# A decoder layer on one core: one store moved to another DMA queue, one gate product moved into an earlier head, two output products cut in half

## The chip, the cores and the metric

The kernel runs on one core of a Trainium2 chip. The metric is device time in microseconds (us) for one execution of the whole layer, median of three runs. A separate execution was profiled; its trace gives the start and the length of every instruction, what each one waited for, and when DMAs were issued. In what follows PE is the matrix engine, ACT the activation engine, DVE the vector engine, POOL the general-purpose engine, and SP the engine that does nothing here but issue DMAs. POOL issues DMAs too, from a queue of its own.

## The reference, cut to what matters

One layer over 1024 tokens of width 1024, in float32: a normed input `h` is projected, three branches are computed and merged by sigmoid gates, and a channel mixer follows. What the change touches is the merge and what feeds it:

```python
proj = h @ w_in
q_d, k_d, v_d, u_p, q_m, gate_logits = split(proj)
a = diff_attention(q_d, k_d, v_d, lam)          # 8 heads, two softmax maps per head
a = rms_norm(a, subln_g) * (1.0 - lam_init)     # per head
y_attn = a @ w_attn_branch
y_pool = multiscale_pool(u_p, ...) @ w_pool_branch
y_mem  = memory_cross_attention(q_m, ...) @ w_mem_branch
gates = sigmoid(gate_logits)                    # three gates of 1024 columns
mix = gates[0] * y_attn + gates[1] * y_pool + gates[2] * y_mem
x = x + rms_norm(mix @ w_out, norm_mix_post)    # then the channel mixer
```

## The kernel before, in words

Every float32 product is made of three matmuls of "high" and "low" parts (`mm3`, L94). A weight that comes from memory as `raw` is split into such parts by one ACT copy and one DVE subtraction (`split`, L83; `wsplit`, L330, loads and splits). The tags `raw`, `wh` and `wl` have two buffers each, and the pages of `product` (L181) take turns in the last two.

The order of work: norms, memory attention, pooling; then the stretch that the code calls `gp` (L609 on), the attention heads (L1009 on), the merge (L1080 on), the output projection, and the channel mixer.

**The merged pool and memory gates, L609 to L629.** For each pair of 128 output columns (`dt` = 0, 2, 4, 6) and each of two branches, `seven` (L204) computes gate logits for both column tiles with seven half-size products instead of eight. It needs two raw weight tiles: `rawg` of the first kind has two buffers and is loaded one `seven` ahead, that of the second has one buffer and can be loaded only when the last page of the `seven` before has been split from it. The gated branch is summed into `mix`, 128x2x1024, and stored to `mixp_d` in DRAM, 1 MB each, four times in all, at L629 from POOL's queue. All loads of this stretch come from SP's queue. Right behind the last of them come the value projections (L634 to L738): `vtmp` (L639) takes a buffer of the same tag `g` as `mix`, so its first writer, the ACT copy at L703, waits until the last store of `mix` has read its source.

**The attention branch's gates.** The eight column tiles of the first gate are made in three places. Tiles 0 and 1 come from a `seven` just before attention (L766 to L768) into `g01`, which is stored at L1021 to L1023. Tile 2 has its weights split there as well (`gate2`, L770); its 48 matmuls of 128x512 are traced by the generator `gate` (L855), which pauses half way through each of two 512-token halves, evicts each half with an ACT copy (L867) and stores it from POOL (L868). One piece of 12 is taken before the first head (L1015), the other three pieces in head 0. Tile 3 is in head 7, tiles 4 to 7 behind the last head (L1089).

**Heads.** A head has four blocks of two rows of 128 queries. For each row `scores` (L877) makes two maps: matmuls into `pss` (two buffers of two banks), a DVE pass that adds the bias and finds the extreme (L901), an ACT exponential (L906). `combine` (L912) joins the maps on DVE, `turn_weights` (L925) transposes on PE and splits, `weigh_values` (L941) multiplies by the values. Heads 1 to 6 also compute the next head's keys (`head_keys`, L829, 48 matmuls of 128x512). `weave` (L259) spreads such fillers evenly over a head's stages. Head 0 has no `head_keys`; its fillers are loads and the rest of gate tile 2.

**What sets the order on an engine.** When the program is built, a planner lays out one fixed instruction order for each engine: it runs through a cost model of its own, takes what is ready in that model, and of several ready instructions the one that was traced first. So a matmul that was traced late can stand early in PE's order, in the place of a wait that the model foresaw, and a load can stand ahead of one traced before it. On the chip each engine, SP's and POOL's queues among them, keeps that order and waits at the head of it. `tc.issue_after(i)` forbids the planner to place the instructions of a block ahead of `i` on `i`'s engine; it adds no wait.

**The merge.** Behind the heads, for each head: `a` (the head's output) and `rb` (its norms, which went through DRAM as `ss_d`, `sum_d` and `r_d`) are loaded, multiplied on DVE and split into `ath` and `atl` (L1092 to L1101); the norms of heads 4 to 7 are computed at L1095, when those of heads 0 to 3 have long been known. Then for each of eight column tiles (L1119) the weights are split, 48 matmuls over all eight heads go into `pya`, and the result is gated, added to `mixp_d` and split into `mixh` and `mixl`.

Of the kernel before, what the change touches and what calls it, by code (L numbers as in the profile page):

```python
# [1 line left out]

# [36 lines left out]
def kernel(  # L39
# [298 lines left out]
    def chunk(w, c0, n=P):  # L338
        return w[:, c0:c0 + n].rearrange("(k p) c -> p k c", p=P)
# [269 lines left out]
    with tc.tile_pool(name="gp", reuse_waits="tile", bufs=2, side="right") as gp_:  # L609
        for dt in range(0, KT, 2):  # L610
            mix = None
            for b in (1, 0):
                raws = []
                for e in range(2):
                    w = (grp if e else wst).tile([P, KT, P], F32, tag="raw", name="rawg", bufs=2 - e)
                    nc.sync.dma_start(out=w, in_=chunk(w_in, C_G + (2 - b) * D + (dt + e) * P))
                    raws.append(w)
                y = gp_.tile([P, 2, S], F32, tag="y", name="y")
                nc.sync.dma_start(out=y, in_=branch_d[b][dt:dt + 2].rearrange("e p s -> p e s"))
                g = gp_.tile([P, 2, S], F32, tag="g", name="g", bufs=3)  # L620
                s12, s43 = [gq.tile([P, 2, H4, P], F32, tag="t", name="s") for _ in range(2)]
                seven(raws, (s12[:, 0], s12[:, 1], s43[:, 0], s43[:, 1]), hop, g)
                sigmoid = nc.scalar.activation(out=g, in_=g, func=AF.Sigmoid)
                nc.vector.tensor_tensor(out=g, in0=g, in1=y, op=ALU.mult)
                if b == 1:
                    mix = g
                else:
                    nc.vector.tensor_tensor(out=mix, in0=mix, in1=g, op=ALU.add)
            nc.gpsimd.dma_start(out=mixp_d[dt:dt + 2].rearrange("e p s -> p e s"), in_=mix)  # L629

# [134 lines left out]
        late = []  # L767
        channels(C_G, ss=[ss[:, j] for j in range(4)], g=g01, late=late)  # L768

        gate2 = wsplit(chunk(w_in, C_G + 2 * P), [P, KT, P])  # L770
        with tc.issue_after(gate2[2].ins):
            late[0]()
    rstack.close()
    tstack.close()
# [79 lines left out]

    def gate(dt):  # L855

        with tc.issue_after(last["load"].ins):
            wh, wl, _ = gate2 if dt == 2 else wsplit(chunk(w_in, C_G + dt * P), [P, KT, P])
        for i in range(2):
            pg = pbank(name="pg0")  # L860
            for k in range(KT):
                if k == H4:
                    yield
                last["gate"] = mm3(pg, wh[:, k, :], wl[:, k, :], hTh[i][:, k, :], hTl[i][:, k, :],
                                   k == 0, k == KT - 1)
            g = gq.tile([P, H], F32, tag="t", name="g0")
            nc.scalar.activation(out=g, in_=pg, func=AF.Copy)  # L867
            nc.gpsimd.dma_start(out=gate_d[dt][:, i * H:(i + 1) * H], in_=g)  # L868
            yield
# [7 lines left out]
    def scores(h, b, u):  # L877

        ks = kts[h]
        t = 2 * b + u  # L880
        n = (t + 1) * P
        parts = 1 if n <= H else 2
        m = n // parts
        q = qts[h, t // 4]
        ts = slice((t % 4) * P, (t % 4 + 1) * P)
        mx = small.tile([P, 2], F32, tag="mx", name="mx")
        sm = small.tile([P, 1], F32, tag="sm", name="sm")
        z2 = []

        def halves(a):  # L890
            return a.rearrange("p (a m) -> p a m", a=parts)

        for c in range(2):
            pss = bank2(name="pss2")
            for i in range(parts):
                keys = ks[c][:, i * m:(i + 1) * m]
                for j in range(2):
                    nc.tensor.matmul(pss[:, i * H:i * H + m], q[:, j, c, ts], keys, start=(j == 0), stop=(j == 1))  # L898
            z = ap_.tile([P, S], F32, tag="z%d" % c, name="z", bufs=3 - c)
            o = 896 - t * P  # L900
            nc.vector.tensor_tensor_reduce(  # L901
                out=halves(z[:, 0:n]), in0=pss.rearrange("p (a m) -> p a m", a=2)[:, 0:parts, 0:m],
                in1=halves(biases[h][:, o:o + n]), scale=1.0, scalar=3.0e38,
                op0=ALU.add, op1=ALU.min, accum_out=mx[:, c:c + 1])
            z2.append(z)
            nc.scalar.activation(out=z[:, 0:n], in_=z[:, 0:n], func=AF.Exp, scale=-1.0,  # L906
                                 bias=mx[:, c:c + 1], accum_out=sm if c else sums[:, h, t:t + 1])
        exps[h, b, u] = z2, mx, sm
        if b == 3 and u == 1:
            kts.pop(h)  # L910
# [95 lines left out]
    def steps(gen, n):  # L1006
        return [lambda: next(gen, None)] * n
# [4 lines left out]
    load_keys(0)  # L1012
    first = gate(2)
    head_bias(0)
    next(first)  # L1015
    for _ in values(0):
        pass
    queries(0, 1)
    load_keys(1)
    last["keys"] = last["load"]  # L1020
    with tc.issue_after(last["load"].ins):  # L1021
        for dt in range(2):
            nc.sync.dma_start(out=gate_d[dt], in_=g01[dt])  # L1023
    GATES = ((2,), (), (), (), (), (), (), (3,))
    blocks = [(h, b) for h in range(NH) for b in range(4)]
    for h in range(NH):
        stages = []
        for b in range(4):
            n = 4 * h + b
            if n == 0:  # L1030
                def first_scores():
                    with tc.issue_after(last["gate"].ins):
                        scores(0, 0, 0)
                stages.append(first_scores)
            else:
                stages.append(lambda h=h, b=b: scores(h, b, 0))
            if b == 1 and h + 1 < NH:
                stages.append(lambda h=h: head_bias(h + 1))
            if n >= 1:
                def weights(n=n):  # L1040
                    combine(*blocks[n - 1], 1)
                    turn_weights(*blocks[n - 1])
                stages.append(weights)
            stages.append(lambda h=h, b=b: scores(h, b, 1))
            stages.append(lambda h=h, b=b: combine(h, b, 0))
            if n >= 2:
                stages.append(lambda n=n: head_norm(*blocks[n - 2]))
            if n >= 1:
                stages.append(lambda n=n: weigh_values(*blocks[n - 1]))
            if h == HG and b == 0:  # L1050
                stages.append(lambda: turn_sums(0))
            if h == HG and b == 1:
                stages.append(lambda: load_norms(0))
            if h == HG and b == 3:
                def norms():
                    with tc.issue_after(last["combine"].ins):
                        head_norms(0)
                stages.append(norms)
            if b in (1, 3) and h + 1 < NH:
                stages.append(lambda h=h, b=b: queries(h + 1, b // 2))  # L1060
        fillers = []
        if h + 1 < NH:
            if h:
                fillers += steps(head_keys(h + 1), 4)
            for n, step in enumerate(steps(values(h + 1), 2)):
                fillers.insert(2 * n + 1, step)
        for dt in GATES[h]:
            fillers += steps(first if dt == 2 else gate(dt), 3 if dt == 2 else 4)
        weave(stages, fillers)
    combine(*blocks[-1], 1)  # L1070
    turn_weights(*blocks[-1])
# [10 lines left out]
    ath = [atp.tile([P, S], F32R, name="ath%d" % h) for h in range(NH)]  # L1082
    atl = [atp.tile([P, S], F32R, name="atl%d" % h) for h in range(NH)]

    with tc.tile_pool(name="sub", reuse_waits="tile", bufs=4, side="right") as sub:
        gs = sub.tile([P, 1], F32, name="gs", bufs=1)
        nc.vector.tensor_scalar(out=gs, in0=cols[:, 1, 44:45], scalar1=1.0 - LAM_INIT, scalar2=None,
                                op0=ALU.mult)
        for dt in range(4, KT):  # L1089
            for step in steps(gate(dt), 4):  # L1090
                step()
        for h in range(NH):  # L1092
            if h == HG:
                with tc.issue_after(ends["square"].ins):
                    head_norms(1)  # L1095
            a = sub.tile([P, S], F32, tag="a", name="a")
            nc.sync.dma_start(out=a, in_=ao_d[h])
            rb = sub.tile([P, S], F32, tag="rb", name="rb")
# [17 lines left out]
        wol.append(pool.tile([P, D], F32R, name="wol%d" % k))  # L1116
        split(woh[k], wol[k], raw)

    for dt in range(KT):  # L1119
        wh, wl, _ = wsplit(chunk(w_attn_branch, dt * P), [P, KT, P])  # L1120
        for i in range(2):
            hs = slice(i * H, (i + 1) * H)
            gm2 = gq.tile([P, 2, H], F32, tag="t", name="gm2")
            g, mp = gm2[:, 0, :], gm2[:, 1, :]
            nc.sync.dma_start(out=g, in_=gate_d[dt][:, hs])
            nc.sync.dma_start(out=mp, in_=mixp_d[dt][:, hs])
            nc.scalar.activation(out=g, in_=g, func=AF.Sigmoid)
            py = (pbank if i else bank)(name="pya")
            for k in range(KT):
                mm3(py, wh[:, k, :], wl[:, k, :], ath[k][:, hs], atl[k][:, hs], k == 0, k == KT - 1)  # L1130
            nc.vector.tensor_tensor(out=g, in0=py, in1=g, op=ALU.mult)
            nc.vector.tensor_tensor(out=g, in0=g, in1=mp, op=ALU.add)
            split(mixh[i][:, dt, :], mixl[i][:, dt, :], g)
    for k in range(4):
        load_wo(woa, k)
    dstack.close()
# [363 lines left out]
```

## Time and profile before

| what | value |
|---|---|
| median of 3 runs | 1768.14 us (1767.33 to 1770.3) |
| profiled execution, its own time | 1771.58 us |
| its span, first to last instruction | 1769.8 us |
| ACT busy | 884.6 us (50%) |
| DVE busy | 1274.3 us (72%) |
| POOL busy | 48.6 us (3%) |
| granted TensorE clock, mean over the span | 0.995 |
| DMA packets | 294.95 MB, mean 167 GB/s |

How to read what is quoted below. A line of the timeline has the start in us, the length in us, the engine, the line of the code, the operation, `out<-in` by the program's names, shape, how many were merged into it, and in brackets how long the engine had been idle and what ended that. A line of the waits has engine and line, what it waited for, then us in total, times, the longest in us. A line of the windows has a stretch, its length, the busy time (and number of instructions) of PE, PE's weight loads, DVE, ACT and POOL, the granted PE clock, the busy share of the 16 DMA engines and GB/s; where a window is restricted to one tile, only the engines that touch it are listed. Matmuls overlap, so a matmul's listed length is more than its share of PE's time; the distance between two starts is that share. A line of the DMA issues has `out<-in`, the queue, how many, KB each, and the median us from issue to landing.

### The profile page before, as it was taken

What the parts mean: (1) busy time and instruction counts of PE and PEld (TensorE: products, weight loads), DVE (VectorE), ACT (ScalarE), POOL (GpSimd) and SP (SyncE); (2) the same over time, 40 slices, a digit from 0 to 9 for tenths busy, and PEclk for the clock granted to TensorE, in tenths of its full rate; (3) what the DMA queues carried; (4) which work ended last, traced back from release to release, by engine and by line L of the source; (5) the groups of instructions that cost most, each with busy time, mean ns of one, the idle gap of its engine ahead of it and who ended that gap; (6) DMA issues with size and microseconds to landing.
All of it is one profiled execution on the core that took longest, in us unless ns stands there. A gap on an engine that the chain in (4) does not pass through costs nothing.

```text
span 1769.8 us, 22658 instructions
## 1 busy us (share of the span) xinstructions
PE 1722.2 (97%) x8138; PEld 1426.2 (81%) x8138; DVE 1274.3 (72%) x2227; ACT 884.6 (50%) x1551; POOL 48.6 (3%) x107
## 2 busy tenths in 40 slices
PE   6999999999899999999999999999999999999997
PEld 5788888777778878888888878888888888788886
DVE  7775875655566567888865557858888888878476
ACT  5434454333444467777753333545555555543452
POOL 0000000000000011111110000000000000000000
PEclk9999999999999999999999999999999999999999
DMA  7783543434784595765556481374334323583343
GB/s 243 249 315 132 180 153 131 126 129 143 228 254 144 188 250 166 192 163 157 157 177 227 157 241 72 111 234 137 108 107 125 115 76 107 185 294 105 112 143 131
DMA packets 232933, 294.95 MB, mean 167 GB/s; under 512 B 15873, under 2 KB 161526, under 8 KB 230134
## 3 DMA queue, kind: packets, MB, share of 16 engines
q1 hardware_dynamic: 228214, 281.94, 50.4%
q0 software_dynamic: 4608, 11.57, 1.8%
q8 instruction: 64, 1.05, 0.3%
q14 instruction: 47, 0.39, 0.1%
HBM read 201.62 MB, written 85.56 MB: 162 GB/s over the span
## 4 chain that ended last, share of the span: by engine, by line
PE 80%; DVE 9%; DMA 5%; ACT 3%; issue 2%; SPq 0%; DVEq 0%; ACTq 0%; POOLq 0%
PE pa L95 7%; PE pa L97 7%; PE pa L96 7%; PE pb L95 5%; PE pb L97 5%; PE pb L96 5%; PE pss L898 2%; PE poa L953 2%; PE pe L96 2%; PE pe L95 2%; PE pe L97 2%; PE pya L95 2%; PE pya L97 2%; PE pya L96 2%; PE pd L95 2%
## 5 line engine op out<-in xcount | busy, mean ns | idle before, releaser
L86 ACT ACTIVATE wpage<-s 128x512 fp32r<-128x512 f32 x136 | 85.2, 626 | 113.1 <-DVE s L194 44.6
L87 DVE TENSOR_TENSOR wpage<-s,wpage 128x512 fp32r<-128x512 f32 x136 | 92.8, 689 | 45.3 <-ACT wpage L86 45.2
L1278 DVE SCALAR_TENSOR_TENSOR cvt<-gv,cols,cvt 128x1023 f32<-128x1023 f32 x88 | 112.5, 1278 | 15.6 <-ACT cvt L1274 15.6
L901 DVE CUSTOM_DVE_ANT_0 z<-pss,hbias 128x256 f32<-128x256 f32 (+7 forms) x128 | 94.9, 753 | 27.4 <-PE pss L898 25.8
L906 ACT ACTIVATE z<-z,mx 128x256 f32<-128x256 f32 (+7 forms) x128 | 99.0, 774 | 19.8 <-DVE mx L901 19.4
L95 PE MATMUL pa<-T,wpage 128*128 128x512 f32 x264 | 102.9, 390 | 1.6 <-DVE gv L252 1.6
L96 PE MATMUL pa<-T,wpage 128*128 128x512 f32 x264 | 102.7, 389 | 0.0
L97 PE MATMUL pa<-T,wpage 128*128 128x512 f32 x264 | 102.7, 389 | 0.0
L898 PE MATMUL pss<-ks,q 128*128 128x512 f32 (+5 forms) x384 | 89.4, 352 | 1.3 <-DVE mx L901 1.1
L86 ACT ACTIVATE page<-blk 128x1024 fp32r<-128x1024 f32 (+1 forms) x42 | 41.4, 988 | 86.2 <-PE pe L96 50.6
L87 DVE TENSOR_TENSOR page<-blk,page 128x1024 fp32r<-128x1024 f32 (+1 forms) x42 | 47.6, 1133 | 38.9 <-ACT page L86 38.8
L86 ACT ACTIVATE wh<-raw 128x1024 fp32r<-128x1024 f32 (+1 forms) x46 | 41.9, 910 | 67.3 <-issue 16.5
L898 PEld LDWEIGHTS pss<-ks,q 128*128 128x128 f32 x384 | 63.3, 190 | 12.4 <-DVE mx L901 7.7
L95 PE MATMUL pa<-hT,wpage 128*128 128x512 f32 x168 | 66.3, 394 | 7.3 <-ACT wpage L86 7.3
L95 PE MATMUL pd<-page 128*128 128x512 f32 x176 | 68.6, 390 | 1.7 <-ACT row L1388 1.7
L96 PE MATMUL pd<-page 128*128 128x512 f32 x176 | 68.5, 389 | 0.0
L97 PE MATMUL pd<-page 128*128 128x512 f32 x176 | 68.5, 389 | 0.0
L97 PE MATMUL pa<-hT,wpage 128*128 128x512 f32 x168 | 66.0, 393 | 0.0
L96 PE MATMUL pa<-hT,wpage 128*128 128x512 f32 x168 | 65.9, 392 | 0.0
L953 PEld LDWEIGHTS poa<-aT,v 128*128 128x128 f32 x480 | 61.3, 192 | 3.9 <-ACT srow L973 1.6
L953 PE MATMUL poa<-aT,v 128*128 128x256 f32 (+1 forms) x480 | 64.0, 283 | 0.0
L87 DVE TENSOR_TENSOR wl<-raw,wh 128x1024 fp32r<-128x1024 f32 (+1 forms) x46 | 47.6, 1035 | 18.3 <-ACT wh L86 18.0
(416 smaller groups left out, 5056.7 us busy)
## 6 DMA issues: line engine op xcount, KB each, us to landing
q<-q_d SPq DMA_DIRECT2D x64, 256.0 KB, 5.5
wd<-in_w_down_dram SPq DMA_DIRECT2D x22, 512.0 KB, 5.2
tw_d<-wd SPq DMA_DIRECT2D x11, 1024.0 KB, 4.6
rawv<-in_w_up_dram SPq DMA_DIRECT2D x22, 512.0 KB, 5.8
rawu<-in_w_up_dram SPq DMA_DIRECT2D x22, 512.0 KB, 4.0
ff_d<-cvt SPq DMA_DIRECT2D x22, 512.0 KB, 4.4
blk<-ff_d SPq DMA_DIRECT2D x20, 512.0 KB, 7.5
br<-tw_d SPq DMA_DIRECT2D x20, 512.0 KB, 3.7
```

The lines of the kernel that those rows point to most:

```text
L86: copy = nc.scalar.activation(out=hi, in_=src, func=AF.Copy)
L87: nc.vector.tensor_tensor(out=lo, in0=src, in1=hi.bitcast(F32), op=ALU.subtract)
L95: nc.tensor.matmul(o, ah, bh, start=first, stop=False, skip_group_check=onto)
L96: nc.tensor.matmul(o, ah, bl, start=False, stop=False, skip_group_check=onto)
L97: return nc.tensor.matmul(o, al, bh, start=False, stop=last, skip_group_check=onto)
L898: nc.tensor.matmul(pss[:, i * H:i * H + m], q[:, j, c, ts], keys, start=(j == 0), stop=(j == 1))
L901: nc.vector.tensor_tensor_reduce(out=halves(z[:, 0:n]), in0=pss.rearrange("p (a m) -> p a m", a=2)[:, 0:parts, 0:m], in1=halves(biases[h][ ...
L906: nc.scalar.activation(out=z[:, 0:n], in_=z[:, 0:n], func=AF.Exp, scale=-1.0, bias=mx[:, c:c + 1], accum_out=sm if c else sums[:, h, t:t + 1])
L953: nc.tensor.matmul(po[:, qs], (vh, vl)[i][:, k, :], w[j][:, ws], start=(n == 0), stop=(n == len(terms) - 1))
L1278: nc.vector.scalar_tensor_tensor(out=cv[:, sh:], in0=u[:, 0:S - sh], scalar=w, in1=cv[:, sh:], op0=ALU.mult, op1=ALU.add)
```

## The change

Four edits.

- The store of `mix` (L629) is issued by SP instead of POOL.
- Gate tile 3 moves from head 7 to head 0, tile 4 from behind the heads to head 7, so that tiles 5 to 7 remain behind them. Tile 3's weights are loaded and split before head 0, ahead of the stores of `g01`. `gate` now pauses after every two of its eight `k`, 6 matmuls at a time; two such pieces (12 matmuls, as before) are taken before head 0.
- Each gate matmul is put behind the last matmul of the newest `scores` (`issue_after`), and the pieces are inserted among a head's fillers from the front, at every second place, instead of being appended.
- Column tiles 0 and 1 of the merge are begun over heads 0 to 3 (`merge_heads(dt, 0)`, 48 matmuls for the two) before the loop comes to head 4; the other half of each follows when all heads are there. Their four banks and two weight buffers are held in between. Tiles 2 to 7 are computed in two halves in a row.

```diff
-            nc.gpsimd.dma_start(out=mixp_d[dt:dt + 2].rearrange("e p s -> p e s"), in_=mix)
+            nc.sync.dma_start(out=mixp_d[dt:dt + 2].rearrange("e p s -> p e s"), in_=mix)
...
-        gate2 = wsplit(chunk(w_in, C_G + 2 * P), [P, KT, P])
-        with tc.issue_after(gate2[2].ins):
+        ready = {2: wsplit(chunk(w_in, C_G + 2 * P), [P, KT, P])}
+        with tc.issue_after(ready[2][2].ins):
             late[0]()
...
         with tc.issue_after(last["load"].ins):
-            wh, wl, _ = gate2 if dt == 2 else wsplit(chunk(w_in, C_G + dt * P), [P, KT, P])
+            wh, wl, _ = ready.pop(dt) if dt in ready else wsplit(chunk(w_in, C_G + dt * P), [P, KT, P])
         for i in range(2):
             pg = pbank(name="pg0")
             for k in range(KT):
-                if k == H4:
+                if k in (2, 4, 6):
                     yield
-                last["gate"] = mm3(pg, wh[:, k, :], wl[:, k, :], hTh[i][:, k, :], hTl[i][:, k, :],
-                                   k == 0, k == KT - 1)
+                with tc.issue_after(last["scores"].ins) if "scores" in last else nullcontext():
+                    last["gate"] = mm3(pg, wh[:, k, :], wl[:, k, :], hTh[i][:, k, :], hTl[i][:, k, :],
+                                       k == 0, k == KT - 1)
...
-                    nc.tensor.matmul(pss[:, i * H:i * H + m], q[:, j, c, ts], keys, start=(j == 0), stop=(j == 1))
+                    last["scores"] = nc.tensor.matmul(pss[:, i * H:i * H + m], q[:, j, c, ts], keys,
+                                                      start=(j == 0), stop=(j == 1))
...
-    next(first)
+    for _ in range(2):
+        next(first)
...
     with tc.issue_after(last["load"].ins):
+        ready[3] = wsplit(chunk(w_in, C_G + 3 * P), [P, KT, P])
         for dt in range(2):
             nc.sync.dma_start(out=gate_d[dt], in_=g01[dt])
-    GATES = ((2,), (), (), (), (), (), (), (3,))
+    GATES = ((2, 3), (), (), (), (), (), (), (4,))
...
+        n = 0
         for dt in GATES[h]:
-            fillers += steps(first if dt == 2 else gate(dt), 3 if dt == 2 else 4)
+            for step in steps(first if dt == 2 else gate(dt), 6 if dt == 2 else 8):
+                fillers.insert(min(n, len(fillers)), step)
+                n += 2
         weave(stages, fillers)
...
+    pys = {}
+
+    def merge_heads(dt, g):
+
+        if g == 0:
+            pys[dt] = wsplit(chunk(w_attn_branch, dt * P), [P, KT, P])[:2] + (bank(name="pya"), pbank(name="pya"))
+        wh, wl, *py = pys[dt]
+        for i in range(2):
+            hs = slice(i * H, (i + 1) * H)
+            for k in range(g * HG, (g + 1) * HG):
+                mm3(py[i], wh[:, k, :], wl[:, k, :], ath[k][:, hs], atl[k][:, hs], k == 0, k == KT - 1)
...
-        for dt in range(4, KT):
-            for step in steps(gate(dt), 4):
+        for dt in range(5, KT):
+            for step in steps(gate(dt), 8):
                 step()
         for h in range(NH):
             if h == HG:
                 with tc.issue_after(ends["square"].ins):
                     head_norms(1)
+
+                for dt in range(2):
+                    merge_heads(dt, 0)
...
-    for dt in range(KT):
-        wh, wl, _ = wsplit(chunk(w_attn_branch, dt * P), [P, KT, P])
-        for i in range(2):
+    def merge(dt):
+
+        for i, py in enumerate(pys.pop(dt)[2:]):
             hs = slice(i * H, (i + 1) * H)
...
-            py = (pbank if i else bank)(name="pya")
-            for k in range(KT):
-                mm3(py, wh[:, k, :], wl[:, k, :], ath[k][:, hs], atl[k][:, hs], k == 0, k == KT - 1)
             nc.vector.tensor_tensor(out=g, in0=py, in1=g, op=ALU.mult)
             nc.vector.tensor_tensor(out=g, in0=g, in1=mp, op=ALU.add)
             split(mixh[i][:, dt, :], mixl[i][:, dt, :], g)
+
+    for dt in range(KT):
+        if dt >= 2:
+            merge_heads(dt, 0)
+        merge_heads(dt, 1)
+        merge(dt)
```

More of the change, by code (lines that the diff above doesn't have):

```diff
@@ L1 @@
-from contextlib import ExitStack
+from contextlib import ExitStack, nullcontext
 import concourse.bass as bass
```

## The prediction

> **What bounds the kernel now.** I read the page's head first, then the windows of 25 us, then who PE waited for, then the timeline around each place where PE stood.
>
> ```profile
> span 1769.8 us, 22658 instructions
> PE 1722.2 (97%) x8138; PEld 1426.2 (81%) x8138; DVE 1274.3 (72%) x2227; ACT 884.6 (50%) x1551; POOL 48.6 (3%) x107
> ...
> PE pa L95 <- ACT wpage L86: 7.3, 4, 3.3
> PE ve L95 <- ACT vpage L86: 3.9, 1, 3.9
> PE pta L936 <- DVE aT L87: 1.8, 3, 0.9
> PE pn L971 <- DVE aT L87: 1.4, 1, 1.4
> ```
>
> PE is the bound. The change takes no matmul away and adds none, so it can only fill or shorten stretches in which PE waits or runs slowly. Those it touches are the first two rows of waits (around the mix stores) and the last two (head 0).
>
> ```profile
> 366.00:371.00 5.00, 5.00 (x16) 3.93 (x16) 3.21 (x6) 1.49 (x3) 0.00 (x0) 0.66 0.00 0
> 448.00:456.00 8.00, 6.59 (x15) 4.90 (x16) 4.86 (x6) 3.55 (x7) 0.00 (x0) 0.57 0.43 135
> ...
> 633.00:656.00 23.00, 22.86 (x124) 18.60 (x122) 18.27 (x53) 16.44 (x41) 2.22 (x4) 1.00 0.85 228
> 656.00:673.00 17.00, 13.57 (x84) 11.57 (x85) 13.57 (x39) 13.06 (x34) 2.68 (x5) 0.90 0.50 166
> ...
> 862.00:906.00 44.00, 43.32 (x262) 36.79 (x263) 34.07 (x81) 30.74 (x73) 6.45 (x12) 1.00 0.32 90
> 906.00:944.00 38.00, 38.00 (x170) 31.39 (x170) 24.95 (x36) 15.33 (x19) 4.32 (x8) 1.00 0.86 302
> ```
>
> Behind waits PE's granted clock drops: 5 x 0.34 = 1.7 us lost at 366, 8 x 0.43 = 3.4 at 448, 17 x 0.10 = 1.7 in head 0. Head 0 has 17 - 13.57 = 3.4 us of idle PE, all in its second half; head 7 has 0.7, the stretch behind the heads none.
>
> **The mix stores, first to third.**
>
> ```profile
> 293.93 2.49 SPq L616 DMA_DIRECT2D rawg<-in_w_in_dram  x2
> 301.82 0.69 DVE L194 TENSOR_TENSOR s<-rawg 128x512 f32<-128x512 f32 x1 [1.49 <-DMA rawg<-in_w_in_dram]
> ...
> 310.83 2.28 DVE L628 TENSOR_TENSOR g<-g 128x2048 f32<-128x2048 f32 x1
> 313.71 0.88 POOL L629 DMA_DIRECT2D mixp_d<-g  x1 [261.94 <-DVE wpage L87]
> 313.75 1.72 SPq L616 DMA_DIRECT2D rawg<-in_w_in_dram  x2
> 322.66 0.69 DVE L194 TENSOR_TENSOR s<-rawg 128x512 f32<-128x512 f32 x1 [5.35 <-DMA rawg<-in_w_in_dram]
> 323.27 0.68 DVE L221 TENSOR_TENSOR g<-pa,g 128x512 f32<-128x512 f32 x1
> 324.10 0.47 PE L95 MATMUL pa<-hT,wpage 128*128 128x512 f32 x1 [2.75 <-ACT wpage L86]
> 365.75 0.47 PE L95 MATMUL pa<-hT,wpage 128*128 128x512 f32 x1 [3.32 <-ACT wpage L86]
> 406.43 0.47 PE L95 MATMUL pa<-hT,wpage 128*128 128x512 f32 x1 [0.72 <-ACT wpage L86]
> 314.50:316.50 2.00, 2.00 (x11) 1.65 (x10) 1.12 (x2) 0.55 (x1) 0.09 (x1) 1.00 0.63 160
> 316.50:321.50 5.00, 4.85 (x22) 3.69 (x20) 0.81 (x2) 0.08 (x1) 0.00 (x0) 1.00 1.02 361
> ```
>
> The second raw load holds L194; behind L194 on DVE stands L221, which empties the bank that PE's next product adds to. Without a store beside it the load takes 301.82 - 296.42 = 5.4 us from the end of its issue, with one 322.66 - 315.47 = 7.2. So the store costs 1.8 us, and that would be all to gain per stall.
>
> On SP the store comes when `mix` is ready (313.11). The raw loads are issued at 313.75 and 315.1, so by the order of readiness they are queued behind it on SP, and DVE waits for the second. Then the same 2 MB pass the same engines before the load is in. What is won is DMA time unused today while POOL's store gets going: in 314.5 to 316.5 the share is 0.63, 2 x 0.37 = 0.7 us. Bounds: the load's 5.4 us plus the store's 1 MB at the 361 GB/s of the full stretch (2.9) less its lead of 2.0 gives 6.3, a gain of 0.9 (the lead is 315.47 - 313.11, less an issue's own length, which I take as 0.4, between nothing and the 0.73 each of the pair at 634.84); with SP's own median for a 1 MB store (5.0, below) counted in full it is 8.4, a loss of 1.2. I take 0.7 for each of the first two, nearer to the engine share that was seen, and 0.6 for the third, whose whole stall is 0.72: **-2.0 us**. If the planner put the store behind the loads, it would be up to -1.8, -1.8, -0.7.
>
> [...]
>
> **The fourth mix store.**
>
> ```profile
> 433.74 2.74 SPq L644 DMA_DIRECT2D vw<-in_w_in_dram  x2
> 436.58 0.72 POOL L629 DMA_DIRECT2D mixp_d<-g  x1 [37.85 <-DVE g L628]
> 443.12 2.36 DVE L681 TENSOR_TENSOR vw<-vw 128x1024 f32<-128x1024 f32 x2 [0.80 <-DMA vw<-in_w_in_dram]
> 446.78 2.07 ACT L703 ACTIVATE vtmp<-vd 128x512 f32<-128x512 f32 x4 [6.88 <-DMA mixp_d<-g]
> 449.41 0.79 PE L95 MATMUL ve<-vpage,hTh 128*128 128x512 f32 x1 [3.94 <-ACT vpage L86]
> ...
> q_d<-hl SPq DMA_DIRECT2D x8, 1024.0 KB, 5.0
> mixp_d<-g POOLq DMA_DIRECT2D x4, 1024.0 KB, 7.6
> ```
>
> Here ACT itself waits: `vtmp` takes the buffer that the store reads, four copies stand for 6.9 us, and the pages PE needs (L86) stand behind them. POOL's store is issued after the last `vw` load and beside two `rawk` loads, and lands after 446.7 - 436.6 = 10.1 us. On SP it needs the same L628 as the last `vw` load and was traced first, so it goes first, at the latest at 433.74 + 2.74 = 436.5: landing 441.5, copies done 2.1 later, by 444. The price is that the last `vw` comes up to 2.9 us later (443.1 to 446.0), and DVE's pair L681 (2.36) and one low page (0.7, as other 128x512 passes on DVE) behind it: PE then goes on at 445.5 to 446.5 with one matmul and fully at 446.0 + 2.4 + 0.7 = 449.1 at the latest, where it now does at 449.4 and 0.7 after. Gain 1.0 to 4 (the whole wait); I take **-2.5**, between, since both ends come from rows of equal nearness.
>
> The clock losses at 366 and 448, together 5.1 us, hang on those stalls. I take half, **-2.5** (bounds 0 and 5.1), because the stalls get shorter but do not vanish. [...]
>
> **Head 0.**
>
> ```profile
> 633.00:656.00 23.00, 11.68 (x38) 6.52 (x36) 0.58 (x1) 1.00 0.85 228
> ...
> 634.84 1.47 SPq L1023 DMA_DIRECT2D gate_d<-g  x2
> 654.41 0.58 ACT L867 ACTIVATE g<-pg 128x512 f32<-128x512 f32 x1
> 656.83 0.55 PE L936 MATMUL pta<-ident,z 128*128 128x128 f32 x3 [0.85 <-DVE aT L87]
> 658.75 0.51 PE L971 MATMUL pn<-sq,ones 128*128 128x256 f32 x2 [1.37 <-DVE aT L87]
> ...
> 944.41 0.40 PE L95 MATMUL pya<-ath,wh 128*128 128x512 f32 x1
> 944.64 0.40 PE L96 MATMUL pya<-atl,wh 128*128 128x512 f32 x1
> ```
>
> The first row is restricted to `pg`: tile 2's remaining 36 matmuls are all used up by 656, and the gaps come after that. Two starts lie 0.23 us apart (last rows), so tile 3 brings 48 x 0.23 = 11 us of work for 3.4 us of gaps, and none of it can run before the scores it is tied to. That leaves some 0.4 us of gaps: -3.0, and -1.7 of clock. The moved tile's load (512 KB, SP, ahead of the stores at 634.84) and split fall into a stretch with DMA share 0.85; by the diff it is kept behind the loads of heads 0 and 1. Ties take fillers from the first microseconds: +0.8 there, my choice. Together **-3.9**. The bound above: the ACT copy of tile 2's first half needs a buffer that the stores at 634.84 read; now it stands 16 us behind its product (654.41), so nothing waits. Its piece is traced earlier now; put at about 638, with the stores landing near 646 (a landing as long as that of the stalled store above, 10.1 us), ACT would stand 8 us, of which 24 gate matmuls cover 5.5: +2.5 and 1.7 of clock, so this term reaches from -5.1 to +4.2.
>
> **Head 7 and the merge.** Tile 4 in place of tile 3 in head 7 costs nothing by count; the ties may open gaps beside the 0.7 there: +0.4 (0 to +2). Behind the heads one gate of 48 matmuls goes and 48 of the half tiles come, so the cover of the last norms is as long as before.
>
> ```profile
> 927.60 2.44 DVE L87 TENSOR_TENSOR atl<-a,ath 128x1024 fp32r<-128x1024 f32 x2
> 942.80 1.04 ACT L86 ACTIVATE ath<-a 128x1024 fp32r<-128x1024 f32 x1
> ```
>
> Heads 0 to 3 are split by 930.0, and PE comes to them at 944.4 - 11 = 933.4. Head 7's high part is ready at 943.8; PE wants it 21 matmuls after 944.4 now (949.2), and 9 after it then (946.5). Weight loads that now come last go ahead of the late `a` and `rb`: two of 512 KB at 302 GB/s are 3.5 us, so up to +0.8 of wait and 1.7 of clock; I take +0.5.
>
> **Sum.** -2.0 - 2.5 - 2.5 - 3.9 + 0.4 + 0.5 = -10.0 on the profiled execution's 1771.58: 1761.6. That one lies 3.4 us above the median of 1768.14, and clock drops are the only part of it that need not be in every run, so for the median I count the clock terms (4.2) at half: -7.9, **1760.2 us**.
>
> **Rivals.**
> [...]
> - *Head 0 is not filled* (the tied pieces stand behind ACT's copies, which free the banks): store terms alone, -5.75 + 0.9: 1763.3. For it: the copy at 654.41. Against: 11 us of work for gaps after 656.
> - *Slower: the loads stand behind the whole store.* In SP's queue both raw loads follow the store. If it holds the engines for over 1.8 + 2.0 = 3.8 us, each stall grows; with the full 5.0 by 1.2, thrice, the fourth by 1.1 (`vw` 5.0 later), and one more clock drop, 1.7: +6.4, against head 0's -3.05 + 0.9: 1772.4. Against: 1 MB at 361 GB/s takes 2.9.
> - *It does nothing that counts*: planner and phase eat both parts: about 1768.
>
> **Chances.** A run of this kernel can tell about 0.2% from no change, 3.5 us. The forecast 0.47; head 0 not filled 0.15, and 0.03 of better cases: faster 0.65. The store only changes place 0.15, nothing that counts 0.06: same 0.21. Behind the whole store 0.10, ACT stalled in head 0 or the late merge outweighing the rest 0.04: slower 0.14. The range goes from 1750 (stalls 1 to 3 nearly closed, most of the clock back) to 1769.
>
> **What would show it.** Right: in the mix stretch L703 waits under 3 us for `mixp_d`, no PE wait over 3 us; second half of head 0 with `pg` rows and under 1 us of PE idle; no gap at the first `pya`. Wrong: `rawg` to L194 over 7.2 us; an ACT wait for `gate_d` between 636 and 650; a PE wait at `pya` on `ath`.

## The result, and the profile after

| what | before | after |
|---|---|---|
| median | 1769.22 us (4 runs) | 1746.57 us (4 runs, 1744.85 to 1747.3) |
| profiled execution | 1771.58 us | 1744.85 us |
| span | 1769.8 us | 1742.8 us |

The ratio is 0.9867, with a 95% interval from 0.9847 to 0.9888: 20 to 27 us faster. The forecast was 8 us less (1760.2), so the direction was right and the size far too small. The head of the page of after:

```profile
span 1742.8 us, 22648 instructions
PE 1711.0 (98%) x8138; PEld 1421.4 (82%) x8138; DVE 1272.8 (73%) x2227; ACT 884.7 (51%) x1551; POOL 45.4 (3%) x103
```

The windows over the mix and value stretch, of after and then of before:

```profile
300.00:480.00 180.00, 178.30 (x780) 145.70 (x779) 118.17 (x151) 82.61 (x129) 0.00 (x0) 1.00 0.52 168
```

```profile
300.00:480.00 180.00, 168.21 (x715) 136.35 (x714) 108.58 (x136) 72.63 (x113) 3.06 (x4) 0.97 0.45 144
```

In the same 180 us the kernel gets through 780 matmuls instead of 715. PE is idle 1.7 us of them instead of 11.8, and the clock is whole instead of 0.97, some 5 us more. Most of the result lies here. Starts of the same instructions in the two traces give the account by stretch (gate matmuls that changed place are taken off at 0.2267 us each, the usual distance of two starts):

| stretch | forecast, on the profiled execution | the two traces |
|---|---|---|
| up to the mix stretch (not touched) | 0 | -1.4 |
| mix stretch up to the first value product | -2.0, clock -0.8 | -9.2 |
| values up to the first scores | -2.5, clock -1.7 | -8.2 |
| the heads | -3.5 | -6.5 |
| behind the heads up to the output projection | +0.5 | +0.3 |
| the rest (not touched) | 0 | -2.0 |
| sum | -10.0 | -27.0 |

The profiled execution of after is itself 1.7 us faster than its median, that of before 2.4 slower; so the two traces lie 27.0 apart and the medians 22.7, and 3.4 of the 27.0 fall in stretches that the change does not touch. At the first of the stalls the timeline of after has, on SP, on DVE and on PE:

```profile
311.70 0.37 SPq L629 DMA_DIRECT2D mixp_d<-g  x1
313.65 1.28 SPq L616 DMA_DIRECT2D rawg<-in_w_in_dram  x2
...
317.22 0.69 DVE L221 TENSOR_TENSOR g<-pa,g 128x512 f32<-128x512 f32 x1 [1.36 <-PE pa L97]
319.18 0.69 DVE L194 TENSOR_TENSOR s<-rawg 128x512 f32<-128x512 f32 x1 [1.27 <-DMA rawg<-in_w_in_dram]
...
319.51 0.39 PE L97 MATMUL pc<-hTh,wpage 128*128 128x512 f32 x1
319.74 0.39 PE L95 MATMUL pa<-hT,wpage 128*128 128x512 f32 x1
```

Three things differ from before. The store goes first, as forecast. The load that L194 waits for is now the first of the pair at 313.65, where it was the second. And L221, which empties PE's bank, stands ahead of L194: DVE still waits for the load, but PE no longer waits for DVE. The planner laid out the second and the third anew; a listing of the orders that it laid out for both kernels shows it at all three places (the first, cut to these two instructions of DVE):

```
+L221 TENSOR_TENSOR g_2778<-pa_2785,g_2778 128x512
 L194 TENSOR_TENSOR s_2909<-rawg_2904 128x512
-L221 TENSOR_TENSOR g_2778<-pa_2785,g_2778 128x512
```

At the fourth store ACT's wait fell from 6.9 to 1.9 us (the timeline of after, SP and ACT):

```profile
425.50 0.37 SPq L629 DMA_DIRECT2D mixp_d<-g  x1
425.91 0.46 SPq L644 DMA_DIRECT2D vw<-in_w_in_dram  x1
...
431.15 2.07 ACT L703 ACTIVATE vtmp<-vd 128x512 f32<-128x512 f32 x4 [1.88 <-DMA mixp_d<-g]
```

And in the first head, 610 to 680, PE's waits of after are:

```profile
PE pg L95 <- ACT g L869: 0.6, 1, 0.6
PE pss L900 <- DVE mx L904: 0.3, 1, 0.3
PE pta L939 <- DVE aT L87: 0.2, 1, 0.2
```

### The profile page after: what moved, and what is told of

Same layout as the page of the kernel before. It is cut to its first block, busy times and chain, and to the rows that moved or that the text cites. A ratio compares the mean times of both kernels' runs of the same rounds, so it can differ in the third digit from the quotient of the medians.

```text
span 1742.8 us, 22648 instructions
## 1 busy us (share of the span) xinstructions
PE 1711.0 (98%) x8138; PEld 1421.4 (82%) x8138; DVE 1272.8 (73%) x2227; ACT 884.7 (51%) x1551; POOL 45.4 (3%) x103
## 4 chain that ended last, share of the span: by engine, by line
PE 85%; DVE 7%; DMA 4%; ACT 2%; issue 2%; SPq 0%; DVEq 0%; ACTq 0%
PE pa L95 8%; PE pa L97 8%; PE pa L96 8%; PE pb L95 5%; PE pb L97 5%; PE pb L96 5%; PE pss L900 3%; PE poa L956 2%; PE pe L95 2%; PE pe L97 2%; PE pe L96 2%; PE pya L96 2%; PE pya L95 2%; PE pya L97 2%; PE pd L95 2%; PE pd L97 2%
## 5 line engine op out<-in xcount | busy, mean ns | idle before, releaser
L904 DVE CUSTOM_DVE_ANT_0 z<-pss,hbias 128x256 f32<-128x256 f32 (+7 forms) x128 | 94.4, 752 | 25.7 <-PE pss L900 24.6
```

Source lines behind the costliest of these rows:

```text
L904: nc.vector.tensor_tensor_reduce(out=halves(z[:, 0:n]), in0=pss.rearrange("p (a m) -> p a m", a=2)[:, 0:parts, 0:m], in1=halves(biases[h][ ...
```

## The experiments

For the first edit there were two theories. *Order*: what closes the three stalls is that the planner, given the store in SP's queue, arranged DVE differently. *Queue*: it is the earlier landing. The edit does both at once, so they were taken apart. The kernels of a group ran on the same chip as runs of the kernel before, whose median was 1769.6 to 1770.9; differences and intervals are against those.

### The store alone

```diff
-            nc.gpsimd.dma_start(out=mixp_d[dt:dt + 2]...
+            nc.sync.dma_start(out=mixp_d[dt:dt + 2]...
```

> The kernel before with the mix store in SP's queue and nothing else. Both theories of the first edit (the new order that the planner gives DVE and SP; the queue itself) expect the whole of it: the three stalls at the raw loads and the fourth store's stall gone with their clock losses, 9.2 and 8.2 us earlier at the first value product and at the first scores, in all 17 us less than before (15 to 19). If the edits hang together, less than 12.

Measured: 1752.48, 17.1 less (ratio 0.9887 to 0.9918), as expected. This one line carries three quarters of the result. DVE's rows of the timeline have the new order here too, and PE's waits in 300 to 480 have none on `pa`:

```profile
316.84 0.69 DVE L221 TENSOR_TENSOR g<-pa,g 128x512 f32<-128x512 f32 x1 [1.36 <-PE pa L97]
318.56 0.69 DVE L194 TENSOR_TENSOR s<-rawg 128x512 f32<-128x512 f32 x1 [1.02 <-DMA rawg<-in_w_in_dram]
```

### DVE's order alone

```diff
-        nc.vector.tensor_tensor(out=s1, in0=a21, in1=a22, op=ALU.add)
+        with tc.issue_after(emptied["add"].ins) if emptied.pop("tie", 0) else nullcontext(): nc.vector.tensor_tensor(out=s1, in0=a21, in1=a22, op=ALU.add)
...
-        nc.vector.tensor_tensor(out=c22, in0=pa, in1=c21, op=ALU.add)
+        emptied["add"] = nc.vector.tensor_tensor(out=c22, in0=pa, in1=c21, op=ALU.add)
...
-                raws = []
+                raws, emptied["tie"] = [], b == 0 and dt > 0
```

> The kernel before, stores on POOL; only DVE's order is changed, at the three places: L221, which empties PE's bank, is tied ahead of L194, which waits for the raw load. Order theory: PE stands under 0.5 us at all three places although L194 waits for its load as long as before, the half clock at 367 is gone, the values start 7 to 9 us earlier, the fourth store stalls as before: 8 us less in all (6 to 10). Queue theory: the late load holds up T1's page instead of L221, PE stands as long a few us later, and the time is that of before within 2 us.

Measured: 1762.91, 6.7 less (0.9946 to 0.9971). DVE's rows of the timeline, then PE's waits in 300 to 480:

```profile
318.13 0.69 DVE L221 TENSOR_TENSOR g<-pa,g 128x512 f32<-128x512 f32 x1 [1.36 <-PE pa L97]
322.18 0.69 DVE L194 TENSOR_TENSOR s<-rawg 128x512 f32<-128x512 f32 x1 [3.35 <-DMA rawg<-in_w_in_dram]
```

```profile
PE ve L95 <- ACT vpage L86: 3.1, 1, 3.1
PE pa L95 <- ACT wpage L86: 2.4, 2, 1.3
```

The load is as late as before (9.6 us after the mix's end, against 9.5), and PE does not stand there. The 2.4 us are two new waits, at 341 and 381, in the `seven` behind, where PE now arrives earlier and the load of L194 does not come earlier by as much: part of the gain is given back later. (The waits' view names ACT, which had long been done; it is L221 behind L194 again.)

### SP's order alone

The load that L194 waits for is issued first of the pair, by the same kind of tie on SP; the store stays on POOL.

> The kernel before, stores on POOL, DVE's order as before; only SP's order is changed: the raw load that L194 waits for is issued ahead of the other one (the order that SP has in the changed kernel), which moves it by one issue of 1.35 us. Order of SP as the cause: the stalls of 2.75 and 3.3 fall to 1.4 and 2.0, the third stays at 0.7: 2.7 us less, up to 4.4 with the clock at 367. Order of DVE or the queue as the cause: under 3 us less and no stall gone.

Measured: 1765.30, 4.3 less (0.9965 to 0.9988). SP's and DVE's rows, then PE's waits in 300 to 480:

```profile
314.55 1.94 SPq L616 DMA_DIRECT2D rawg<-in_w_in_dram  x2
...
321.22 0.69 DVE L194 TENSOR_TENSOR s<-rawg 128x512 f32<-128x512 f32 x1 [4.46 <-DMA rawg<-in_w_in_dram]
321.83 0.68 DVE L221 TENSOR_TENSOR g<-pa,g 128x512 f32<-128x512 f32 x1
```

```profile
PE ve L95 <- ACT vpage L86: 4.6, 1, 4.6
PE pa L95 <- ACT wpage L86: 4.5, 3, 1.9
```

The three stalls sum to 4.5 us, against this line of before:

```profile
PE pa L95 <- ACT wpage L86: 6.8, 3, 3.3
```

They are shorter and none is gone, as the theory of SP's order has it; but the load is not issued earlier, as was expected. In both kernels it goes out 2.0 us after the mix's end (315.10 - 313.11 before, 314.55 - 312.57 here). What changes is the other load, which before went out 1.35 us ahead of it and now stands behind it.

### SP's queue, with DVE's old order

```diff
-        nc.vector.tensor_tensor(out=c22, in0=pa, in1=c21, op=ALU.add)
-        product(a12, op, "B21", pc)
+        w12, w22 = (page(a12), page(a22)) if ahead else (None, None)
+        with tc.issue_after(ahead()) if ahead else nullcontext():
+            nc.vector.tensor_tensor(out=c22, in0=pa, in1=c21, op=ALU.add)
+        product(a12, op, "B21", pc, w=w12)
...
```

`ahead()` traces the next loads and the next L194, so that L221 can be tied behind it; for that the last two weight pages of a `seven` are traced earlier too, and the first two products of the next are tied behind its last matmul. The lines of this kernel are shifted: L200 is the L194 of the others, L233 their L221.

> Stores on SP as in the changed kernel, SP's new order too, but DVE's old order at the three places: L194 ahead of L221. Order theory: the stalls come back, shorter by the 2.0 us by which the load lands earlier after the mix is ready: 0.8, 1.3 and 0 instead of 2.75, 3.3 and 0.7; with the fourth store's 8.2 that is 13 us less than before (11 to 15), 2 to 4 more than with the store on SP alone. Queue theory: no stall is left, the same time as the store on SP alone, 17 less than before.

Measured: 1754.57, 15.0 less (0.9898 to 0.9925). DVE's rows, then PE's waits in 300 to 480:

```profile
320.05 0.69 DVE L200 TENSOR_TENSOR s<-rawg 128x512 f32<-128x512 f32 x1 [3.07 <-DMA rawg<-in_w_in_dram]
320.65 0.68 DVE L233 TENSOR_TENSOR g<-pa,g 128x512 f32<-128x512 f32 x1
```

```profile
PE pa L95 <- ACT wpage L86: 2.2, 4, 1.3
```

With the kernel before, these make a square and a fifth case. For each, the time from the mix's end (L628) to the start of the waiting L194 and to L221 at the first two places, and PE's waits on `pa` in 300 to 480:

| store, DVE's order | L194 | L221 | waits | median |
|---|---|---|---|---|
| POOL, old (before) | 9.5, 10.1 | 10.2, 10.7 | 6.8 | 1769.6 |
| POOL, old, load first | 8.7, 8.7 | 9.3, 9.3 | 4.5 | 1765.3 |
| POOL, new | 9.6, 9.7 | 5.6, 5.6 | 2.4 | 1762.9 |
| SP, old | 7.3, 8.1 | 7.9, 8.7 | 2.2 | 1754.6 |
| SP, new | 7.3, 8.1 | 5.6, 5.6 | 0 | 1752.5 |

So the order theory is right about the mechanism (the stalls with the old order on SP came out at 0.5, 1.3 and 0, expected 0.8, 1.3 and 0; the rest of the 2.2 are two of 0.2 at 341 and 381) and wrong as the main cause: either half alone takes most of the stalls away, and together they leave nothing. On SP the load is in 2.3 and 2.0 us earlier; 0.9 and 1.4 of that comes with the order of the two loads, and the rest, 1.4 and 0.6, with the store being out of their way.

### The fourth store alone

```diff
+            (nc.sync if dt == KT - 2 else nc.gpsimd).dma_start(out=mixp_d[dt:dt + 2]...
```

> The kernel before with the fourth mix store alone in SP's queue, the first three on POOL as before. Theory: the stalls at the raw loads stay (2.9, 3.5, 0.9 us, half clock at 367), the fourth store goes ahead of the last vw load and frees vtmp's buffer before ACT wants it; 4.3 us of PE stall and 3.4 of half clock go: 7.5 to 9 us less than before. The prediction on record has 2.5 and half of the clock for it, 4.2 in all. Rival: part of the gain hangs on the first three stores' shift, then under 5.

Measured: 1764.56, 6.4 less (0.9953 to 0.9978). ACT's and DVE's rows, then PE's waits in 300 to 480:

```profile
443.78 2.07 ACT L703 ACTIVATE vtmp<-vd 128x512 f32<-128x512 f32 x4 [1.99 <-DMA mixp_d<-g]
...
446.97 1.23 DVE L681 TENSOR_TENSOR vw<-vw 128x1024 f32<-128x1024 f32 x1 [1.50 <-DMA vw<-in_w_in_dram]
448.12 1.29 DVE L87 TENSOR_TENSOR vpage<-vw,vpage 128x512 fp32r<-128x512 f32 x2
```

```profile
PE pa L95 <- ACT wpage L86: 7.1, 4, 3.4
PE ve L95 <- ACT vpage L86: 0.5, 2, 0.3
```

The first three stalls stand as before, the fourth is gone: it does not hang on the others. The last `vw` load is later by 446.97 - 443.12 = 3.9 us, 1.9 of which this run already had at the first value product; but one L681 where two stood is now between that load and the page, which starts 1.3 us earlier than before (449.39), 3.1 without those 1.9. Expected were 7.5 to 9 us. By the starts, the stretch from the first value product to the first scores is 7.7 us shorter than before (8.2 in the changed kernel). The 6.4 of the median are less, with an interval from 4 to 8; the profile shows one reason, half clock at two other places, told in the last section.

### The store on a third queue

The changed kernel with `nc.scalar.dma_start` at L629.

> The changed kernel with the mix store in ACT's queue instead of SP's. Quick start theory (the gain is that the store's data move before the loads', whichever queue issues it, if it starts as soon as SP's does): the changed kernel's time within 2 us (1747 to 1751), no PE wait over 1 us from 300 to 480. In-order theory (the gain needs the loads behind the store in the same queue): store and loads share the engines, the load lands 1 to 2 us later, and ACT, which holds the pages behind the store's wait for L628, adds to it: 2 to 6 us more (1750 to 1755).

Measured: 1750.99, 19.1 less (0.9871 to 0.9909). That lies in both expected ranges, and the interval overlaps with that of the changed kernel (0.9847 to 0.9888), so the time does not decide. The traces do, and differently at the first three stores and at the fourth. SP's, DVE's and ACT's rows, then PE's waits in 300 to 480:

```profile
311.84 3.96 SPq L616 DMA_DIRECT2D rawg<-in_w_in_dram  x2
...
317.90 0.69 DVE L221 TENSOR_TENSOR g<-pa,g 128x512 f32<-128x512 f32 x1 [1.89 <-PE pa L97]
320.42 0.69 DVE L194 TENSOR_TENSOR s<-rawg 128x512 f32<-128x512 f32 x1 [0.24 <-DMA rawg<-in_w_in_dram]
...
433.89 1.57 ACT L703 ACTIVATE vtmp<-vd 128x512 f32<-128x512 f32 x3 [4.36 <-DMA mixp_d<-g]
```

```profile
PE ve L95 <- ACT vpage L86: 1.5, 1, 1.5
```

At the first three stores no stall follows, since L221 stands ahead. L194 comes as late as with POOL, 9.2 us after the mix's end at the first, but the store is not what holds it: the load that it waits for is the second of the pair again and goes out only at 315.43, 4.2 us after the mix's end instead of 2.0, and is in 5.0 us later, against 5.5 in the changed kernel and 7.6 before. So here the store need not stand in the loads' own queue; it is enough that it starts early. In the packets of the traces POOL's first data move 3.3 and 3.2 us after the issue at the first two stores of before, ACT's 1.4 at both of this run. The fourth store, issued at 425.72 beside the loads and not ahead of them, frees `vtmp`'s buffer at 433.9, 8.2 us later; on SP it takes 431.15 - 425.50 = 5.7. There the place in SP's queue counts: PE stands 1.5 us, and the clock is 0.93 from 420 to 445.

### Edits two to four alone

The changed kernel with the store back on POOL.

> The changed kernel with the mix store back on POOL: edits two to four alone. Theory, from the traces: head 0 gives 5.8, the rest 0.5, so 6 us less than before (5 to 8), and the stalls of the mix stretch are all there. Prediction on record for these parts: 3.9 less, 0.9 more, 3.0 in all.

Measured: 1763.44, 7.5 less (0.9951 to 0.9976). That is within the 5 to 8 expected. With the 17.1 of the store it makes 24.6, against 22.7 together: no interplay that the intervals show.

### The first head: amount or placement

Without the second tile in head 0:

```diff
-        ready[3] = wsplit(chunk(w_in, C_G + 3 * P), [P, KT, P])
...
-    GATES = ((2, 3), (), (), (), (), (), (), (4,))
+    GATES = ((2,), (), (), (), (), (), (), (3,))
...
-        for dt in range(5, KT):
+        for dt in range(4, KT):
```

> The changed kernel with its small tied pieces, but without the second gate tile in the first head: tile 3 goes to head 7 and tile 4 behind the heads, as in the kernel before. Amount theory (the gaps of the first head want more work): tile 2's 8 us of pieces are used up before the head ends or leave its last third bare, 3 to 5 us come back with the clock, 1750 to 1752. Placement theory (the gaps want work that is still there late): the small tied pieces of tile 2 alone close them, the changed kernel's time within 1 us.

With it, in the old pieces, behind the other fillers, not tied:

```diff
-                if k in (2, 4, 6):
+                if k == H4:
...
-                with tc.issue_after(last["scores"].ins) if "scores" in last else nullcontext():
+                with nullcontext():
...
-            for step in steps(first if dt == 2 else gate(dt), 6 if dt == 2 else 8):
-                fillers.insert(min(n, len(fillers)), step)
-                n += 2
+            fillers += steps(first if dt == 2 else gate(dt), 3 if dt == 2 else 4)
```

> The changed kernel with tile 3 in the first head, but the gate pieces as in the kernel before: of 12 matmuls, put behind the other fillers, not tied to the scores. Amount theory: 11 us more of work for 3 to 5 us of gaps is enough however it is cut, the changed kernel's time within 1.5 us. Placement theory: pieces that the planner may spend early leave the second half bare again, 3 to 5 us more than the changed kernel, 1750 to 1752.

The changed kernel beside them:

> The changed kernel unaltered, on the same chip as the two above, to set them against: 22 us less than before (20 to 25), on every theory.

Measured: 1751.58 without the tile (19.2 less than before), 1748.85 with the tile alone (21.9), 1748.73 unaltered (22.0). The waits of PE in 610 to 680, first without the tile, then with the tile alone:

```profile
PE pss L900 <- DVE mx L904: 1.4, 4, 0.5
PE pta L939 <- DVE z L923: 1.3, 3, 0.7
PE pta L939 <- ACT sq L962: 0.3, 1, 0.3
```

```profile
PE pta L939 <- DVE aT L87: 1.2, 1, 1.2
PE pss L900 <- DVE mx L904: 0.2, 1, 0.2
```

Amount it is, for the most part. Without the tile the gaps are cut small and spread, but their sum is 3.0, near the 3.4 of before. The first two heads, from the first scores to the last value matmul of head 1 and less their gate matmuls, take 65.0 us before, 63.4 without the tile, 60.8 with the tile alone, 60.0 changed. By that the tile is worth 3.4 to 4.2 us, the cut and the ties 0.8 to 1.6; in the medians the tile is worth 2.7 to 2.9, and the cut and the ties 0.1.

### Without the ties

```diff
-                with tc.issue_after(last["scores"].ins) if "scores" in last else nullcontext():
+                with nullcontext():
```

> The changed kernel without the ties of the gate matmuls to the scores. Theory: without ties the planner spends the gate work in the first microseconds of the head, the gaps of its second half come back in part, 2 to 4 us more than the changed kernel (1749 to 1751). Rival, from the prediction on record: the ties cost 0.8 us in the first microseconds, then 0.8 less (1746).

Measured: 1748.04 (0.9859 to 0.9889), between the two expectations and within the uncertainty of the changed kernel; in the trace the first two heads take 60.4 us, against 60.0 and 60.2 in the two profiles with ties. The ties do not cost the 0.8 of the prediction, and that they bring anything is not shown: over all eight heads this kernel takes 1.5 us more than the changed one, but so does the kernel with the store back on POOL, which has the ties.

### Without the half output tiles

```diff
-                for dt in range(2):
-                    merge_heads(dt, 0)
...
-        if dt >= 2:
-            merge_heads(dt, 0)
+        merge_heads(dt, 0)
```

> The changed kernel without the half output tiles: behind the heads come three gate tiles and then the output tiles, whole, as in the kernel before, which had four gates there. Theory: the half tiles stand in for the gate tile that went into the heads, so without them the last heads' norms are 11 us short of cover: PE stands some 3 to 6 us at the first output tile on ath, with up to 1.7 of clock: 3 to 7 us more than the changed kernel (1750 to 1754). Rival: the norms were ready early enough all along, then the same within 1 us.

Measured: 1754.30 (0.9888 to 0.9915), 6 to 8 more than the changed kernel (6.2 by the ratios, 7.7 by the medians), at the upper end; but the theory named the wrong wait. POOL's and SP's rows, then PE's waits in 915 to 950, then a window:

```profile
922.54 0.54 POOL L870 DMA_DIRECT2D gate_d<-g  x1 [6.46 <-ACT g L869]
...
927.11 0.32 SPq L1146 DMA_DIRECT2D gm<-gate_d  x1
927.95 1.06 SPq L333 DMA_DIRECT2D raw<-in_w_attn_branch_dram  x2
```

```profile
PE pya L95 <- ACT wh L86: 3.4, 1, 3.4
PE pya L95 <- ACT ath L86: 0.6, 1, 0.6
```

```profile
935.00:940.00 5.00, 4.61 (x14) 3.64 (x15) 4.63 (x6) 2.02 (x3) 0.00 (x0) 0.66 0.35 106
```

PE waits 0.6 us for `ath`, and 3.4 for weights: their load stands on SP behind that of `gate_d` (L1146), and that one takes a buffer (tag `t`) from which POOL still stores half of the last gate tile, issued at 922.54. At a clock of 0.66, 1.7 us more go. It is the case of `vtmp` and the fourth store again. In the changed kernel the half tiles stand over this time, and PE has no wait from 890 to 960.

## Why the prediction was right or wrong

**What bounds the kernel, and the direction**: right. PE's waits and the clock behind them were most of what the change touched, and the store was the larger part. All its signs for "right" are there: L703 waits 1.9 us, no PE wait is over 3 us in the mix stretch, the second half of head 0 (from 637) has a wait of 0.2 and `pg` pieces in it, and there is none at `pya`.

**The first three stores** (forecast -2.0, and -0.8 of clock; measured -9.2 with the clock): the step that failed. It read that the second raw load holds L194 and that L221 stands behind L194, both right for before, and carried both into the new kernel. It then priced only the DMA time that POOL's late start leaves unused, 0.7 us. That term was about right: with the store out of the way the load is in 1.4 and 0.6 us earlier at the first two places. But the change also moved the store in the planner's model, and the planner swapped the two loads (0.9 and 1.4 us earlier) and put L221 ahead of L194 (which by itself brings the waits from 6.8 to 2.4 us). The section on the kernel before says that the planner fixes each engine's order by its own model; the working used that for the store alone.

**The fourth store** (forecast -2.5, of 1 to 4, and -1.7 of clock; measured -8.2 with the clock): the mechanism right, the size too small. PE's wait of 3.9 us at `ve` fell to 0.5 with this store alone. The price, a last `vw` load up to 2.9 us later with DVE's pair L681 behind it, came as a load some 2 us later with half of the pair: the planner had moved the other, which does not need that load, ahead of it. Again it was an order, taken over from before.

**The clock in the mix and value stretch** (half of 5.1): all of it came back in the profiles (1.00 over 300 to 480, where before has 0.97), in which the stalls vanished instead of shrinking. That half of it would stay with shorter stalls was the author's estimate; no run shows it, and the last section has the same gaps with a loss and without one.

**Head 0** (-4.7 before the ties, the loss by ties 0.8): the first two heads gained 5.0, and the loss by ties is not there. That the sum came out is luck in part. The half clock in head 0, counted at 1.7, was worth 0.3 (the last section shows it), so the gaps brought 4.7, where 3.0 were forecast. With the whole clock they are wider than the 3.4 us that the prediction read: PE's waits in this stretch sum to 4.4 in the kernel with the fourth store alone. What brings the rest stays open. The bound on the bad side, ACT behind the stores of `g01`, did not occur. Another 1.5 us in heads 2 to 7 is in the changed kernel's two profiles and not in the kernel with the store back on POOL, whose first two heads gained as much; what makes it stays open.

**Head 7 and the merge** (+0.9): +0.3 behind the heads. "Costs nothing by count" holds, for a reason that the prediction had not: the half tiles cover a load of weights more than the norms (waits of 3.4 and 0.6 us without them).

**The rivals**: "the store only changes place", by which all three store terms are nil, is out. From 316.5 to 321.5 before, with the loads and the store under way together, the DMA share was 1.02, and still the move was worth 17 us (17.1 with the store alone): it decided which transfer went first and when, and with that what the planner built around it. "The loads stand behind the whole store" is out too: they do, and land earlier. So is "head 0 is not filled", by the 5.0 us of the first two heads, and with them "nothing that counts".

## What to carry to other kernels

When a program builds its own instruction order, an edit to one DMA can reorder other engines: get the new order listed before pricing the edit, and price the order, not the transfer alone. At a stall that goes "load, then an add that needs it, then an add that frees PE's bank", ask first whether the second add can stand ahead; here that was worth about as much as an earlier load (waits of 2.4 and 2.2 us instead of 6.8). For gaps in a stretch, count the work that can be there before thinking about how finely to cut it.

## What the runs showed of the hardware

**Half clock came in pieces.** In the trace of before the granted clock is 1.00 up to 1760 but for three pieces at 0.50: 3.41 us from 367.05, 6.83 from 448.97 and 3.41 from 660.60. In that of after it is 1.00 up to 1735. The 0.90 over the 17 us of head 0 before is one such piece, averaged over a longer window:

```profile
660.60:664.01 3.41, 3.07 (x16) 2.78 (x15) 2.04 (x5) 3.38 (x8) 0.57 (x1) 0.50 1.01 376
```

**The same gaps brought a piece in one run and none in another.** Six of the kernels have head 0 as it was before, with the same order on PE. In before, the store alone, the fourth store alone and DVE's order alone PE waits 0.8 to 0.9 us for `pta` and 1.4 for `pn` at the same place. Four of the six drop to half clock in head 0: before and the load first (0.94 over 650 to 680), the store alone and SP with DVE's old order (0.93 over 625 to 650). Two, the fourth store alone (1.00 over 630 to 670) and DVE's order alone (1.00 over 625 to 680), keep the whole clock. The fourth store alone has its pieces elsewhere: one behind the first stall, where before has none, and two instead of one behind the second:

```profile
323.91:327.32 3.41, 3.41 (x10) 2.63 (x9) 2.10 (x4) 0.44 (x1) 0.00 (x0) 0.50 0.00 0
364.87:371.69 6.82, 5.76 (x14) 4.59 (x15) 4.51 (x8) 1.53 (x3) 0.00 (x0) 0.50 0.00 0
```

**In head 0 a later wait took most of the piece back.** PE's rows in head 0, of before and then of the fourth store alone:

```profile
658.75 0.51 PE L971 MATMUL pn<-sq,ones 128*128 128x256 f32 x2 [1.37 <-DVE aT L87]
663.25 0.69 PE L936 MATMUL pta<-ident,z 128*128 128x128 f32 x2 [0.34 <-DVE z L920]
```

```profile
652.88 0.51 PE L971 MATMUL pn<-sq,ones 128*128 128x256 f32 x2 [1.37 <-DVE aT L87]
657.39 0.44 PE L936 MATMUL pta<-ident,z 128*128 128x128 f32 x2 [1.30 <-DVE z L920]
```

Both come to the matmul that needs DVE's `z` 4.5 us after `pn`. At half clock PE comes later and waits 0.34 us there instead of 1.30. Counted from the first scores, the kernel with the whole clock is only 0.3 us ahead in the rest of head 0 and in head 1, not 1.7. Behind the first stall of the mix stretch no such wait follows, and there the piece costs the fourth store alone 1.6 us by the starts.

So in these profiles a clock loss was no property of the stall. A term for it belongs into a forecast as a chance, and by these two places at full price only where PE waits for nothing soon after. A long wait was not needed either: in the kernel with the load first the clock is 0.91 over 355 to 375, one piece, where PE's longest wait is 1.9 us.
